# Residual of the first two w_o groups by accumulating transfers, (0,0) of the other two by VectorE, and S1 of the last SwiGLU's first two groups put together by transfers

## The chip, the cores and the metric

The kernel runs on one core of a Trainium2 chip. The metric is the device time of one execution in microseconds. A core has TensorE (the profile writes PE for its matmuls and PEld for its weight loads), VectorE (DVE), ScalarE (ACT), GpSimd (POOL) and SyncE (SP). Each of them works through its own instructions strictly in the order in which they were issued to it. Transfers are issued from SP's queue (plain copies) and from POOL's queue (here: copies that add to what stands in the destination), and are carried by 16 DMA engines that all queues share.

## What is computed

One encoder block over 1024 tokens of width 1024, all in float32:

```python
h = h + 0.5 * swiglu_ffn(rmsnorm(h, norm_ffn1), ffn1_w_in, ffn1_w_out)
u = rmsnorm(h, norm_mix)
...                                   # retention and pooling branches, gates
merged = gate[:, :, 0] * (ret @ w_ret_up) + gate[:, :, 1] * (pool_out @ w_pool_up)
h = h + merged @ w_out
h = h + 0.5 * swiglu_ffn(rmsnorm(h, norm_ffn2), ffn2_w_in, ffn2_w_out)
return rmsnorm(h, norm_final)

def swiglu_ffn(x, w_in, w_out):
    gate, up = split(x @ w_in, 2)
    return (silu(gate) * up) @ w_out
```

The change is about the line with `w_out` (the kernel calls the matrix w_o), its residual addition, and the first products of the last SwiGLU with `ffn2_w_in`.

## The kernel before

**Products.** All large matrix products are done in blocks of 2 by 2 by Strassen's method in Winograd's form: seven block products instead of eight. `strassen` (L479) makes one group: a pair of 128-row weight tiles (`wa`, `wb`, each 128 x 1024, halves L11, L12, L21, L22) against an operand whose sums (R11, R12, T1, T2, T3, T4 and so on) are shared by all groups of a stage. The weights of a group need their own sums: S1 = L21 + L22, S2 = S1 - L11, S3 = L11 - L21, S4 = L12 - S2. A group has seven steps, numbered 0 to 6: L11 x R11, S2 x T2, S1 x T1, S3 x T3, L12 x R21, S4 x R22, L22 x T4. Since TensorE here multiplies in a reduced form of float32, each factor is split into a high part (a cast by ScalarE, L164) and a low part (a subtraction by VectorE, L165), and each product is three matmuls: high x high (L184), high x low (L185) and low x high (L186). A step is 4 x 3 matmuls.

**Results of a group.** Four blocks (tile, half): (0,0) after step 4, (1,1) after steps 2 and 3, (1,0) after step 6, (0,1) after step 5. `evac` adds what lies in PSUM and what was set aside, and writes the block to SBUF. (0,0) and (0,1) come out of PSUM whole; (1,0) and (1,1) are a sum of PSUM and of a set-aside piece. After step 0 the bank `a` is copied by ScalarE into a bank `b` (L530) before step 4 may go on adding to `a`.

**The stage around the change.** `merge` (L1908) runs the four groups of the branch projection (tiles ru0 to ru3, operand "ru"), then the four groups of w_o (`out_group`, L1855, tiles wo0 to wo3, operand "mg", made of the ru tiles), then the last SwiGLU begins (`ffn_in`, groups c0, c11, c1, c12, ..., operand "n3", made of the wo tiles; "n3ssq" collects the squares for its norm). `two_by_two` (L707) takes the groups in pairs and goes through the steps in the order BY_OPERAND = 0, 4, 1, 3, 2, 6, 5, each step for both groups of the pair. The weights of a step are prepared LOOK = 4 steps ahead. `handed` (L1886) puts the making of the next operand into the list of side work (`Flow`), which is emptied two items per step; `m` numbers in it are steps again (0: R11, 4: R21, 1: T2, 3: T3, 2: T1, 6: T4, 5: R22). `rest` is the part that is left to the end of the second pair.

**The residual of w_o.** The block is added to h1 (in HBM). Two ways are in use: the old values are loaded by SP into the block's place in the tile beforehand, and VectorE adds to them (L1879, for blocks of two pieces also L1881); or the block is written without them (ScalarE's copy L1875, VectorE's sum L1873), and a transfer from POOL's queue adds h1 to it (`onto`), after which the next step of the block (`ffn2.quarter`: store to h2, square, sum of squares) must wait; it is kept in `waiting` until `handed` releases it. Before, the second way is used for (0,0) of all four groups and for (1,1) of groups 2 and 3.

**What sets the order.** The names above say in which order work is given out; a scheduler then moves instructions within each engine's queue by its own costs and priorities (evacuations are marked urgent), so the order on each engine is that of the built program. Weight tiles have 5 buffers, raw weight tiles 4 (`raw`), tiles of tag `tl` 4.

Of the kernel before, what the change touches and what calls it, by code (L numbers as in the profile page):

```python
# [21 lines left out]
H = S // 2  # L22
DFF = 2816
FT = DFF // P
FH = FT // 2
# [65 lines left out]
def block_kernel(ctx: ExitStack, tc, x, x_tok, x_two, vecs, f1_in, f1_out, w_in, w_v, pool_w, w_ret, w_pool, w_o,  # L91
# [384 lines left out]
    class Group(list):  # L476
        pass

    def strassen(nx, wa, wb, name, evac, end, begin=None, shared=(), dest=None):  # L479

        t = {}

        def blocks():
            ra, rb = raw(f"{name}ra"), raw(f"{name}rb")
            load(ra, wa)
            load(rb, wb)
            t.update(L11=half(ra, 0), L12=half(ra, 1), L21=half(rb, 0), L22=half(rb, 1))

        def combine(n, a, b, op):
            t[n] = c2(f"{name}{n}")
            tt(t[n], t[a], t[b], op)

        def prep_w(n):
            def go():
                if n == "L11":
                    blocks()
                elif n in ("S2", "S3") and "S1" not in t:
                    combine("S1", "L21", "L22", ADD)  # L500
                if n == "S2":
                    combine("S2", "S1", "L11", SUB)
                elif n == "S3":

                    t["S3"] = t["L21"]
                    tt(t["S3"], t["L11"], t["L21"], SUB)
                if n == "S4" or 3 in shared and n == "S1":

                    t["S4"] = t["S2"]
                    tt(t["S4"], t["L12"], t["S2"], SUB)  # L510
                t["w", n] = weights(t[n], f"{name}w{n}")

            return go

        def prod(dst, w, m, start, stop):
            for i in range(4):
                mm3(t[dst], parts(t["w", w], i), moving(nx.operand(m, i)), start and i == 0, stop and i == 3)

        def u(n):
            t[n] = c2(f"{name}{n}")  # L520
            return t[n]

        def b1():
            if begin:
                begin()
            t["a"] = bank(f"{name}a")
            prod("a", "L11", "R11", True, False)
            t["b"] = sum_bank(f"{name}b")
            with soon():
                copy(t["b"], t["a"])  # L530

        def b6():
            prod("b", "S2", "T2", False, False)
            with soon():
                copy(u("v"), t["b"])

        def fourth():

            if "b5" in t and "p7" in t:
                with soon():  # L540
                    evac((1, 1), t["b"], t["p7"])

        def b5():
            prod("b", "S1", "T1", False, False)
            t["b5"] = True
            fourth()

        def b7():
            t["e"] = bank(f"{name}e")
            prod("e", "S3", "T3", True, False)  # L550
            with soon():
                copy(u("p7"), t["e"])
            fourth()

        def b2():
            prod("a", "L12", "R21", False, True)
            with soon():
                evac((0, 0), t["a"], None)

        def b3():  # L560
            prod("b", "S4", "R22", False, True)
            with soon():
                evac((0, 1), t["b"], None)

        def b4():
            prod("e", "L22", "T4", False, True)
            with soon():
                evac((1, 0), t["e"], t["v"])

        def last(f):  # L570
            def go():
                f()
                t["ends"] = t.get("ends", 0) + 1
                if t["ends"] == 2:
                    end()

            return go

        g = Group([(prep_w("L11"), b1), (prep_w("S2"), b6), (prep_w("S1"), b5), (prep_w("S3"), b7),
                   (prep_w("L12"), b2), (prep_w("S4"), last(b3)), (prep_w("L22"), last(b4))])  # L580
        g.t, g.name, g.dest = t, name, dest
        g.finish = {3: last(lambda: evac((0, 1), t["b"], dest((0, 1)))), 2: lambda: evac((0, 0), t["a"], dest((0, 0)))}
        return g
# [171 lines left out]
    def ffn_in(nx, w, ops, name, ahead, start=None):  # L755

        R, T, B, T4 = ops
        hid = {}

        def group(g):  # L760
            gate_up = {}

            def dest(which):
                tile, j = which
                if tile not in gate_up:
                    gate_up[tile] = (tl if start and g == 0 else t4)(f"{name}{'gu'[tile]}{g}")
                return half(gate_up[tile], j)

            later = []

            def evac(which, in0, in1):
                tile, j = which
                dst, rms = dest(which), nx.rb
                if in1 is not None:
                    tt(dst, in0, in1, ADD)
                elif not tile and rms is not None:
                    tt(dst, in0, half(rms, j), MUL)
                    return
                else:
                    copy(dst, in0)  # L780
                if not tile:
                    later.append(j)

            def end():
                gate, up = gate_up[0], gate_up[1]

                def scale():
                    if len(later) == 2:
                        tt(gate, gate, nx.rms(), MUL)
                    else:  # L790
                        for j in later:
                            tt(half(gate, j), half(gate, j), half(nx.rms(), j), MUL)

                def times(j):
                    tt(half(up, j), half(gate, j), half(up, j), MUL)

                flow.add(scale, lambda: act(gate, gate, AF.Silu), lambda: times(0), lambda: times(1))
                hid[g] = up
                k = g % FH
                if g < FH:  # L800
                    return
                lo, hi, e = hid.pop(k), up, {}
                R11, R12, R21, R22 = half(lo, 0), half(lo, 1), half(hi, 0), half(hi, 1)

                def w1():

                    e["n"], e["m"] = gate, c2(f"{name}m{k}")
                    tt(half(e["n"], 0), R12, R11, SUB)

                def w1b():  # L810
                    tt(half(e["n"], 1), R22, R12, SUB)
                    load(B[k], e["n"])

                def w2():
                    tt(R12, R22, half(e["n"], 0), SUB)
                    load(R[k], lo)
                    load(T[k], hi)

                def w3():
                    tt(e["m"], R21, R12, SUB)  # L820
                    load(T4[k], e["m"])
                    done.add(k)

                flow.add(w1, w1b, w2, w3)

            if start and g == 0:
                return plain_group(nx, start, f"{name}{g}_", evac, end)
            return lambda shared: strassen(nx, w[g, 0], w[g, 1], f"{name}{g}_", evac, end, shared=shared, dest=dest)

        done = ops_done.setdefault(name, set())  # L830
        order = [g for k in range(FH) for g in (k, k + FH)]
        if start:

            return chain(group(0), pairs_of_both(nx, (group(g) for g in order[1:]), BY_OPERAND, 3, ahead))
        return pairs_of_both(nx, (group(g) for g in order), BY_OPERAND, 2, ahead)


# [1017 lines left out]
    def out_group(i):  # L1855
# [3 lines left out]
        def begin():  # L1859
            for z in range(2):  # L1860
                pair[z] = t4(f"{name}{z}")
                if i > 1 or z == 0:
                    load(half(pair[z], 1 - z), half(h1[i + 4 * z], 1 - z))
                else:
                    load(pair[z], h1[i + 4 * z])

        def evac(which, in0, in1):
            tile, j = which
            dst = half(pair[tile], j)
            step = lambda: ffn2.quarter(i + 4 * tile, slice(j * H, (j + 1) * H), pair[tile])  # L1870
            if tile == j and (i > 1 or tile == 0):
                if in1 is not None:
                    tt(dst, in0, in1, ADD)  # L1873
                else:
# [11 lines left out]
    def handed(nx, last):  # L1886
# [1 line left out]
        f = after(nx)  # L1888

        def between(pair, n):  # L1890
            if n in (3, 5):
                flow.add(*waiting)
                waiting.clear()
            if pair == 0:
                if n == BY_OPERAND[-1]:
                    flow.add(*(lambda m=m, i=i: m(i) for i in range(2) for m in (nx.r22, nx.sum1, nx.sum3)))
                return
            flow.add(*(lambda i=i: f[n](i) for i in range(2)))

            for m in {3: (0,), 6: (4,)}.get(n, ()):  # L1900
                flow.add(*(lambda i=i: f[m](i) for i in range(2, 4)))
            if n == BY_OPERAND[-1]:
                rest = [lambda m=m, i=i: f[m](i) for m in (1, 3, 2, 6, 5) for i in range(2, 4)]
                last(rest)

        return between
# [203 lines left out]
```

## Time and profile before

| | us |
|---|---|
| median of 3 runs | 2060.94 |
| lowest, highest run | 2059.88, 2061.10 |
| the profiled execution | 2061.32 |
| its span, first to last instruction | 2059.5 |

The stages that matter, by the first matmul of each in the timeline:

| stretch, us from the start | what runs |
|---|---|
| 1373.6 to 1410.3 | w_o, groups 0 and 1 |
| 1410.3 to 1448.1 | w_o, groups 2 and 3 |
| 1448.1 to 1490.6 | last SwiGLU, groups c0 and c11 |

The page lists busy time, instructions and idle time of each engine. A row of the timeline gives start and duration in us, engine, line, operation, destination<-sources without buffer numbers, shape and count, and in brackets how long the engine had been idle and what ended that. A row of the waits gives the waiting engine, tile and line, then what it waited for, then the sum in us, the number of times and the longest.

### The profile page before, as it was taken

What the parts mean: (1) busy time and instruction counts of PE and PEld (TensorE: products, weight loads), DVE (VectorE), ACT (ScalarE), POOL (GpSimd) and SP (SyncE); (2) the same over time, 40 slices, a digit from 0 to 9 for tenths busy, and PEclk for the clock granted to TensorE, in tenths of its full rate; (3) what the DMA queues carried; (4) which work ended last, traced back from release to release, by engine and by line L of the source; (5) the groups of instructions that cost most, each with busy time, mean ns of one, the idle gap of its engine ahead of it and who ended that gap; (6) DMA issues with size and microseconds to landing.
All of it is one profiled execution on the core that took longest, in us unless ns stands there. A gap on an engine that the chain in (4) does not pass through costs nothing.

```text
span 2059.5 us, 29729 instructions
## 1 busy us (share of the span) xinstructions
PE 2041.1 (99%) x10672; PEld 1810.8 (88%) x10672; DVE 1831.4 (89%) x3253; ACT 1092.0 (53%) x2067; POOL 9.1 (0%) x14
## 2 busy tenths in 40 slices
PE   9999999999999999999999999999999999999998
PEld 7888999988888888888888999888889989998887
DVE  8889998998996798989789987899989989899896
ACT  8545444554754554454447753457645545455454
POOL 0000000000000000000000000010000000000000
PEclk9999999999999999999999999999999999999999
DMA  7332424585543343243336667545233232468642
GB/s 245 138 103 77 144 88 144 200 276 194 189 144 115 101 140 106 92 145 127 110 130 219 205 226 272 193 111 163 80 100 131 88 133 88 136 207 276 210 149 97
DMA packets 120259, 313.57 MB, mean 152 GB/s; under 512 B 13360, under 2 KB 17584, under 8 KB 120112
## 3 DMA queue, kind: packets, MB, share of 16 engines
q1 hardware_dynamic: 118096, 308.01, 43.8%
q0 software_dynamic: 1440, 2.62, 0.8%
q8 instruction: 83, 1.36, 0.3%
q10 hardware_dynamic: 576, 1.05, 0.1%
q14 instruction: 64, 0.52, 0.1%
HBM read 220.93 MB, written 90.70 MB: 151 GB/s over the span
## 4 chain that ended last, share of the span: by engine, by line
PE 84%; DVE 10%; ACT 2%; DMA 2%; issue 2%; SPq 0%; ACTq 0%; DVEq 0%
PE a_b L184 2%; PE a_b L186 2%; PE a_b L185 2%; PE c_b L184 2%; PE c_b L185 2%; PE c_b L186 2%; PE a_e L186 2%; PE c_e L186 2%; PE c_e L184 2%; PE a_e L184 2%; PE c_e L185 2%; PE a_e L185 2%; PE a_a L186 1%; PE a_a L184 1%; PE a_a L185 1%
## 5 line engine op out<-in xcount | busy, mean ns | idle before, releaser
L184 PE MATMUL c_b<-n3T,c_wS 128*128 128x512 f32 x176 | 66.8, 380 | 1.7 <-ACT n3T L164 1.7
L185 PE MATMUL c_b<-n3T,c_wS 128*128 128x512 f32 x176 | 66.8, 380 | 0.0
L186 PE MATMUL c_b<-n3T,c_wS 128*128 128x512 f32 x176 | 66.7, 379 | 0.0
L184 PE MATMUL a_b<-n1T,a_wS 128*128 128x512 f32 x168 | 63.7, 379 | 0.0
L185 PE MATMUL a_b<-n1T,a_wS 128*128 128x512 f32 x168 | 63.7, 379 | 0.0
L186 PE MATMUL a_b<-n1T,a_wS 128*128 128x512 f32 x168 | 63.7, 379 | 0.0
L184 PE MATMUL a_a<-n1R,a_wL 128*128 128x512 f32 x120 | 45.5, 379 | 0.0
L186 PE MATMUL a_a<-n1R,a_wL 128*128 128x512 f32 x120 | 45.5, 379 | 0.0
L185 PE MATMUL a_a<-n1R,a_wL 128*128 128x512 f32 x120 | 45.5, 379 | 0.0
L184 PE MATMUL c_a<-n3R,c_wL 128*128 128x512 f32 x112 | 42.7, 381 | 0.7 <-ACT c_b L530 0.5
L185 PE MATMUL c_a<-n3R,c_wL 128*128 128x512 f32 x112 | 42.4, 379 | 0.0
L186 PE MATMUL c_a<-n3R,c_wL 128*128 128x512 f32 x112 | 42.4, 379 | 0.0
L184 PEld LDWEIGHTS c_b<-n3T,c_wS 128*128 128x128 f32 x176 | 33.3, 189 | 6.6 <-ACT n3T L164 2.1
L185 PEld LDWEIGHTS c_b<-n3T,c_wS 128*128 128x128 f32 x176 | 33.3, 189 | 4.8 <-DVE n3T L165 0.3
L186 PEld LDWEIGHTS c_b<-n3T,c_wS 128*128 128x128 f32 x176 | 33.3, 189 | 4.7
L186 PEld LDWEIGHTS a_b<-n1T,a_wS 128*128 128x128 f32 x168 | 31.8, 189 | 4.5
L184 PEld LDWEIGHTS a_b<-n1T,a_wS 128*128 128x128 f32 x168 | 31.8, 189 | 4.4
L185 PEld LDWEIGHTS a_b<-n1T,a_wS 128*128 128x128 f32 x168 | 31.8, 189 | 4.4
L165 DVE TENSOR_TENSOR a_wS<-a_S,a_wS 128x512 fp32r<-128x512 f32 x45 | 30.6, 682 | 3.6 <-ACT a_wS L164 3.6
L165 DVE TENSOR_TENSOR c_wS<-c_S,c_wS 128x512 fp32r<-128x512 f32 x46 | 31.3, 683 | 2.6 <-ACT c_wS L164 2.6
L184 PE MATMUL c_e<-n3T,c_wS 128*128 128x512 f32 x88 | 33.5, 380 | 0.0
L184 PE MATMUL c_e<-n3T,c_wL 128*128 128x512 f32 x88 | 33.4, 380 | 0.0
(3167 smaller groups left out, 8003.7 us busy)
## 6 DMA issues: line engine op xcount, KB each, us to landing
c_ra<-in_f_in SPq DMA_DIRECT2D x22, 512.0 KB, 3.6
c_rb<-in_f_in SPq DMA_DIRECT2D x22, 512.0 KB, 3.6
a_ra<-in_f_in SPq DMA_DIRECT2D x21, 512.0 KB, 3.7
a_rb<-in_f_in SPq DMA_DIRECT2D x21, 512.0 KB, 3.7
t<-au SPq DMA_DIRECT2D x11, 512.0 KB, 2.8
b<-ag SPq DMA_DIRECT2D x11, 512.0 KB, 3.8
r<-au SPq DMA_DIRECT2D x11, 512.0 KB, 3.5
bra<-in_f_out SPq DMA_DIRECT2D x11, 512.0 KB, 4.8
```

The costliest lines, as they stand in the source:

```text
L165: tt(lo, src, hi.bitcast(F32), SUB)
L184: mm(dst, w[0], m[0], start=start, stop=False, skip_group_check=True)
L185: mm(dst, w[0], m[1], start=False, stop=False, skip_group_check=True)
L186: mm(dst, w[1], m[0], start=False, stop=stop, skip_group_check=True)
```

## The change

In `out_group`, all four blocks of groups 0 and 1 are now written without the residual, and transfers from POOL's queue add it: ten such transfers in w_o instead of six. For groups 2 and 3, (0,0) is now added by VectorE to loaded values, as (0,1) and (1,0) were already; only (1,1) is still by transfer. `handed` releases the waiting blocks at other points, makes the first sums of the n3 operand (r22, sum1, sum3) of groups 0 and 1 later (after step 4 of the second pair and no longer at the end of the first), and puts R22 of groups 0 and 1 into `rest` behind T2 and T3; the last also holds for the mg operand. In `strassen`, the new argument `summed` lets c0 and c11 take S1 from two transfers: one loads L21 of the weights into a half of a `tl` tile (c0_S1), one adds L22, so that VectorE's sum falls away.

```diff
--- before.py
+++ after.py
@@ -476,7 +476,7 @@
     class Group(list):
         pass
 
-    def strassen(nx, wa, wb, name, evac, end, begin=None, shared=(), dest=None):
+    def strassen(nx, wa, wb, name, evac, end, begin=None, shared=(), dest=None, summed=None):
 
 
 
@@ -487,6 +487,13 @@
             load(ra, wa)
             load(rb, wb)
             t.update(L11=half(ra, 0), L12=half(ra, 1), L21=half(rb, 0), L22=half(rb, 1))
+            if summed is not None:
+                if not summed:
+                    s = tl(f"{name}S1")
+                    summed.extend((half(s, 1), half(s, 0)))
+                t["S1"] = summed.pop()
+                load(t["S1"], wb[:, :H])
+                onto(t["S1"], wb[:, H:])
 
         def combine(n, a, b, op):
             t[n] = c2(f"{name}{n}")
@@ -755,7 +762,7 @@
     def ffn_in(nx, w, ops, name, ahead, start=None):
 
         R, T, B, T4 = ops
-        hid = {}
+        hid, halves = {}, []
 
         def group(g):
             gate_up = {}
@@ -825,7 +832,8 @@
 
             if start and g == 0:
                 return plain_group(nx, start, f"{name}{g}_", evac, end)
-            return lambda shared: strassen(nx, w[g, 0], w[g, 1], f"{name}{g}_", evac, end, shared=shared, dest=dest)
+            return lambda shared: strassen(nx, w[g, 0], w[g, 1], f"{name}{g}_", evac, end, shared=shared, dest=dest,
+                                           summed=halves if not start and g % FH == 0 else None)
 
         done = ops_done.setdefault(name, set())
         order = [g for k in range(FH) for g in (k, k + FH)]
@@ -1859,16 +1867,16 @@
         def begin():
             for z in range(2):
                 pair[z] = t4(f"{name}{z}")
-                if i > 1 or z == 0:
+                if i > 1:
                     load(half(pair[z], 1 - z), half(h1[i + 4 * z], 1 - z))
-                else:
-                    load(pair[z], h1[i + 4 * z])
+                    if not z:
+                        load(half(pair[z], z), half(h1[i], z))
 
         def evac(which, in0, in1):
             tile, j = which
             dst = half(pair[tile], j)
             step = lambda: ffn2.quarter(i + 4 * tile, slice(j * H, (j + 1) * H), pair[tile])
-            if tile == j and (i > 1 or tile == 0):
+            if i < 2 or tile and j:
                 if in1 is not None:
                     tt(dst, in0, in1, ADD)
                 else:
@@ -1888,19 +1896,21 @@
         f = after(nx)
 
         def between(pair, n):
-            if n in (3, 5):
+            if (pair, n) in ((0, 3), (1, 4), (1, 5)):
                 flow.add(*waiting)
                 waiting.clear()
-            if pair == 0:
-                if n == BY_OPERAND[-1]:
-                    flow.add(*(lambda m=m, i=i: m(i) for i in range(2) for m in (nx.r22, nx.sum1, nx.sum3)))
+            if (pair, n) == ((1, 4) if nx is ffn2 else (0, BY_OPERAND[-1])):
+                flow.add(*(lambda m=m, i=i: m(i) for i in range(2) for m in (nx.r22, nx.sum1, nx.sum3)))
+            if not pair:
                 return
-            flow.add(*(lambda i=i: f[n](i) for i in range(2)))
+            if n != BY_OPERAND[-1]:
+                flow.add(*(lambda i=i: f[n](i) for i in range(2)))
 
             for m in {3: (0,), 6: (4,)}.get(n, ()):
                 flow.add(*(lambda i=i: f[m](i) for i in range(2, 4)))
             if n == BY_OPERAND[-1]:
-                rest = [lambda m=m, i=i: f[m](i) for m in (1, 3, 2, 6, 5) for i in range(2, 4)]
+                rest = [lambda m=m, i=i: f[m](i) for m, at in ((1, 2), (3, 2), (5, 0), (2, 2), (6, 2), (5, 2))
+                        for i in (at, at + 1)]
                 last(rest)
 
         return between
```

VectorE's rows just ahead of the low part of wo1's S2 weights (wo1wS2), in w_o, groups 0 and 1. mgT.. and mgR22.. are operand parts, wo0rb/wo1S.. sums of weights. Before:

```order
L493 TENSOR_TENSOR wo1S1_13682<-wo1rb_13566 128x512
L165 TENSOR_TENSOR mgT22_13673<-ru20_13295,mgT22_13673 128x512
L165 TENSOR_TENSOR mgT23_13679<-ru30_13331,mgT23_13679 128x512
L493 TENSOR_TENSOR wo1S2_13684<-wo1S1_13682,wo1ra_13565 128x512
L351 TENSOR_TENSOR ru20_13295<-ru21_13297,ru20_13295 128x512
L351 TENSOR_TENSOR ru30_13331<-ru31_13333,ru30_13331 128x512
L165 TENSOR_TENSOR wo1wS2_13686<-wo1S2_13684,wo1wS2_13686 128x512
```

And now:

```order
L165 TENSOR_TENSOR mgT32_13675<-ru20_13295,mgT32_13675 128x512
L351 TENSOR_TENSOR ru30_13331<-ru31_13333,ru30_13331 128x512
L500 TENSOR_TENSOR wo1S1_13682<-wo1rb_13566 128x512
L513 TENSOR_TENSOR wo0rb_13543<-wo0ra_13542,wo0rb_13543 128x512
L165 TENSOR_TENSOR mgT33_13679<-ru30_13331,mgT33_13679 128x512
L500 TENSOR_TENSOR wo1S2_13684<-wo1S1_13682,wo1ra_13565 128x512
L165 TENSOR_TENSOR mgR220_13706<-ru01_12945,mgR220_13706 128x512
L165 TENSOR_TENSOR mgR221_13709<-ru11_12988,mgR221_13709 128x512
L165 TENSOR_TENSOR mgT12_13730<-mgt12_13638,mgT12_13730 128x512
L165 TENSOR_TENSOR wo1wS2_13686<-wo1S2_13684,wo1wS2_13686 128x512
```

Counted from the last row that both programs have in the same place (ru3h01, the gating of ru3's last block), 16 rows stand ahead of wo1wS2 before and 20 now: mgT32, mgT33, wo0rb and mgT12 have come ahead of it, and mgR220 and mgR221, which stood ahead of it anyway, have moved close to it.

ScalarE's rows ahead of the copy of bank a to bank b for wo2 (wo2b<-wo2a). n3q.. and n3ssq are squares of finished wo blocks, wo3wL12 and wo2wS2 high parts of weights. Before:

```order
L291 ACTIVATE n3q4_0_13913<-wo01_13653 128x512
L164 CAST wo2wL12_13941<-wo2ra_13891 128x512
L291 ACTIVATE n3q5_0_13938<-wo11_13691 128x512
L164 CAST wo3wL12_13961<-wo3ra_13916 128x512
L291 ACTIVATE n3q0_512_13958<-wo00_13651 128x512
L291 ACTIVATE n3q1_512_13978<-wo10_13689 128x512
L164 CAST wo2wS2_13986<-wo2S2_13984 128x512
L530 COPY wo2b_14006<-wo2a_13993 128x512
```

And now:

```order
L291 ACTIVATE n3ssq_13839<-wo01_13658 128x512
L164 CAST wo3wL11_13906<-wo3ra_13902 128x512
L164 CAST wo2wL12_13923<-wo2ra_13881 128x512
L346 ACTIVATE wo01_13658<-wo01_13658,vec_66 128x512
L1883 COPY wo00_13657<-wo0b_13672 128x512
L164 CAST wo3wL12_13940<-wo3ra_13902 128x512
L1883 COPY wo10_13689<-wo1b_13704 128x512
L164 CAST wo2wS2_13961<-wo2S2_13959 128x512
L537 COPY wo2b_13982<-wo2a_13969 128x512
```

The four squares of blocks (1,0) and (0,1) have gone to later places; the evacuations of (0,1) of groups 0 and 1 stand there as ScalarE's copies, and the square of wo01 and its scaling, which use a block that a transfer from POOL completes, stand further ahead.

VectorE's rows around the low parts of R21 for tiles 2 and 3 (n3R212, n3R213), at the end of w_o and the start of c0 and c11. Before:

```order
L1879 TENSOR_TENSOR wo31_14020<-wo3e_14152,wo31_14020 128x512
L165 TENSOR_TENSOR c0_wL12_14271<-c0_ra_14223,c0_wL12_14271 128x512
L1881 TENSOR_TENSOR wo31_14020<-wo31_14020,wo3v_14121 128x512
L169 SCALAR_TENSOR_TENSOR n3R212_14373<-wo21_13991,vec_66,n3R212_14373 128x512
L1879 TENSOR_TENSOR wo20_13989<-wo2b_14006,wo20_13989 128x512
L165 TENSOR_TENSOR c11_wL12_14291<-c11_ra_14247,c11_wL12_14291 128x512
L303 TENSOR_TENSOR n3ssq_13843<-n3ssq_13843,n3q7_0_14308 128x512
L493 TENSOR_TENSOR c0_S1_14311<-c0_rb_14224 128x512
```

And now:

```order
L165 TENSOR_TENSOR c11_wS2_14325<-c11_S2_14323,c11_wS2_14325 128x512
L303 TENSOR_TENSOR n3ssq_13839<-n3ssq_13839,n3q7_0_14361 128x512
L392 SCALAR_TENSOR_TENSOR wo11_13690<-wo11_13690,vec_66,wo10_13689 128x512
L165 TENSOR_TENSOR n3T40_14365<-wo01_13658,n3T40_14365 128x512
L165 TENSOR_TENSOR c0_wS3_14347<-c0_rb_14199,c0_wS3_14347 128x512
L165 TENSOR_TENSOR n3T41_14369<-wo11_13690,n3T41_14369 128x512
L169 SCALAR_TENSOR_TENSOR n3R212_14372<-wo21_13967,vec_66,n3R212_14372 128x512
L169 SCALAR_TENSOR_TENSOR n3R213_14378<-wo31_13994,vec_66,n3R213_14378 128x512
```

n3R212 stood ahead of the evacuation of (0,1) of wo2 (wo20<-wo2b); now it stands 12 rows behind that of wo3, and the low parts of c0's and c11's S2 and of T4 come first. TensorE's order has followed: the matmuls with n3R212 and n3R213 of c0 and c11, which were the 31st to the 48th of these groups, now begin with the 36th and end with the 50th, and those with T22 begin with the 78th instead of the 59th, behind T30 and T31 and the sums of squares (n3sum).

## Prediction

> **What bounds the kernel now.** First the page's line of busy times, beside its span:
>
> ```profile
> span 2059.5 us, 29729 instructions
> PE 2041.1 (99%) x10672; PEld 1810.8 (88%) x10672; DVE 1831.4 (89%) x3253; ACT 1092.0 (53%) x2067; POOL 9.1 (0%) x14
> ```
>
> TensorE is busy for 2041.1 of 2059.5 us and the change takes no matmul away, so only TensorE's waits can go. The view of waits for TensorE, cut to 1375 to 1530 us, holds all that lie near the change:
>
> ```profile
> PE c_b L184 <- ACT n3T L164: 1.7, 1, 1.7
> PE wo2a L184 <- ACT wo2b L530: 1.3, 1, 1.3
> PE c_a L184 <- ACT c_b L530: 0.5, 1, 0.5
> PE c_y L184 <- ACT n3R L164: 0.4, 1, 0.4
> PE wo0e L186 <- DVE wo0wS L165: 0.2, 1, 0.2
> ```
>
> They sum to 4.1 us, but matmuls overlap, and a wait costs more than its idle time. The timeline at the second row:
>
> ```profile
> 1415.31 0.38 PE L186 MATMUL wo3a<-mgR,wo3wL 128*128 128x512 f32 x1
> 1416.94 0.48 PE L184 MATMUL wo2a<-mgR,wo2wL 128*128 128x512 f32 x1 [1.25 <-ACT wo2b L530]
> 1417.26 0.38 PE L185 MATMUL wo2a<-mgR,wo2wL 128*128 128x512 f32 x1
> 1417.47 0.38 PE L186 MATMUL wo2a<-mgR,wo2wL 128*128 128x512 f32 x1
> ```
>
> Undisturbed starts are 0.21 to 0.22 apart (1417.26 to 1417.47). Here they are 1.63 apart and then 0.32: lost 1.41 + 0.10 = 1.51, that is the idle time plus 0.26. So the rows cost: c_b 2.0, wo2a 1.5, c_a 0.8, c_y 0.6, wo0e 0.45; a second wait of c_a, too short for this list, is seen below (0.4). **The ceiling of any gain is 5.7 us**, to 2055.6 from the profiled execution's own 2061.3 (span 2059.5 and 1.8 around it). Why these waits are there the view of stretches tells:
>
> ```profile
> 1375.00:1500.00 125.00, 121.17 (x563) 104.08 (x562) 120.19 (x206) 81.91 (x148) 5.23 (x6) 1.00 0.39 117
> ```
>
> The third busy time is VectorE's, 120.19 of 125 us: its queue is full, and ScalarE, whose casts and copies alternate with it in order, is late whenever it is. TensorE's clock is full (1.00).
>
> **The change part by part.** *VectorE's instructions.* For groups 0 and 1, five additions each become two; for groups 2 and 3, four become five; c0 and c11 lose one each. That is 10 + 8 - 4 - 10 + 2 = 6 fewer. Two neighbouring rows give the price:
>
> ```profile
> 1375.24 0.68 DVE L1843 TENSOR_TENSOR ru3h<-ru3b,rg 128x512 f32<-128x512 f32 x1
> 1375.84 0.68 DVE L165 TENSOR_TENSOR mgR<-ru,mgR 128x512 fp32r<-128x512 f32 x1
> ```
>
> One per 0.60 us, so 3.6 us of room on VectorE. It is worth something only where TensorE waits. ScalarE's two (0,0) copies of groups 2 and 3 become two (0,1) copies of groups 0 and 1: nothing in sum.
>
> *wo1's S2 weights: a new wait.* By the order, wo1wS2 moves from the 17th to the 21st row behind ru3h01. VectorE's queue had no gap in this stretch:
>
> ```profile
> 1376.40 0.57 ACT L530 COPY wo0b<-wo0a 128x512 f32<-128x512 f32 x1 [1.78 <-PE wo0a L186]
> 1378.79 0.38 PE L184 MATMUL wo0a<-mgR,wo0wL 128*128 128x512 f32 x1
> 1385.60 0.69 DVE L165 TENSOR_TENSOR wo1wS<-wo1S,wo1wS 128x512 fp32r<-128x512 f32 x1
> 1386.99 0.38 PE L186 MATMUL wo1b<-mgT,wo1wS 128*128 128x512 f32 x1
> 1389.21 0.69 DVE L165 TENSOR_TENSOR wo0wS<-wo0rb,wo0wS 128x512 fp32r<-128x512 f32 x1
> 1389.95 0.48 PE L186 MATMUL wo0e<-mgT,wo0wS 128*128 128x512 f32 x1 [0.18 <-DVE wo0wS L165]
> ```
>
> The last two rows show that a matmul can start 0.74 after its low part starts. So at 1385.60 there were 0.65 to spare (1386.99 - 1385.60 - 0.74), and four rows take 2.4: TensorE waits 1.75. ScalarE adds a little earlier: it must now cast mgT22 before it copies wo0b. Its source is VectorE's third row behind ru3h01 (1375.24 + 3 x 0.60, done 0.7 to 0.8 later at 1377.8); with 0.52 for the cast and 0.57 for the copy the bank is free near 1378.9, where step 4 was due at 1378.79: 0.2 to 0.3, which the wait at wo1b then takes in. Each restart costs 0.1 more (above). Together **+1.8**. The wait at wo0e then goes, since TensorE is late there: **-0.45**.
>
> *The wait at wo2a.* ScalarE's rows ahead of it:
>
> ```profile
> 1413.62 0.75 ACT L291 ACTIVATE n3q<-wo 128x512 f32<-128x512 f32 x1 [1.36 <-DVE wo L1879]
> 1415.78 0.62 ACT L164 CAST wo2wS<-wo2S 128x512 fp32r<-128x512 f32 x1 [1.41 <-DVE wo2S L493]
> 1416.30 0.58 ACT L530 COPY wo2b<-wo2a 128x512 f32<-128x512 f32 x1
> ```
>
> The copy waited behind a square and a cast that waited for VectorE. Now wo2S2 is VectorE's 2nd row behind wo1wS4, some 12 us earlier, and the squares are gone from there; the copy follows TensorE's step 0 of wo2 directly: **-1.5**. What is late next are transfers: ScalarE now stands at n3ssq<-wo01 until POOL's addition to (1,1) of wo0 has landed, and then at wo01's scaling until its store is out.
>
> ```profile
> wo<-h POOLq DMA_DIRECT2D x6, 256.0 KB, 4.0
> h<-wo SPq DMA_DIRECT2D x16, 256.0 KB, 2.0
> wo3rb<-in_w_o SPq DMA_DIRECT2D x1, 512.0 KB, 6.1
> ```
>
> VectorE writes the block near 1400.0, so it lands near 1404.4 and the store near 1406.5; seven ScalarE rows of 0.5 to 0.65 follow (3.7), so the copy could end at 1410.2. TensorE asks for it at 1415.5 + 1.8 - 0.45 = 1416.9. Cover: 6.7 us. In a crowd the additions can take longer; I bound one by 4.0 from below and by 6.1 + 4.0 from above (the wo2 and wo3 weights, 2 MB, are in flight then, and the last of them took 6.1), and take 5: still nothing.
>
> *c0 and c11.* The waits there:
>
> ```profile
> 1447.91 0.38 PE L186 MATMUL wo3b<-mgR,wo3wS 128*128 128x512 f32 x1
> 1451.45 0.68 DVE L1879 TENSOR_TENSOR wo<-wo3b,wo 128x512 f32<-128x512 f32 x1
> 1452.84 0.62 ACT L164 CAST c_wS<-c_S 128x512 fp32r<-128x512 f32 x1 [2.25 <-DVE c_S L493]
> 1453.37 0.58 ACT L530 COPY c_b<-c_a 128x512 f32<-128x512 f32 x1
> 1454.00 0.48 PE L184 MATMUL c_a<-n3R,c_wL 128*128 128x512 f32 x1 [0.53 <-ACT c_b L530]
> 1456.98 0.48 PE L184 MATMUL c_a<-n3R,c_wL 128*128 128x512 f32 x1
> 1463.06 0.62 ACT L164 CAST n3T<-wo 128x512 fp32r<-128x512 f32 x1 [1.72 <-DVE wo L353]
> 1463.73 0.48 PE L184 MATMUL c_b<-n3T,c_wS 128*128 128x512 f32 x1 [1.74 <-ACT n3T L164]
> ```
>
> VectorE takes up wo3's last block at 1451.45, 3.2 us after the bank was full (1447.91 + 0.38). Everything behind inherits that: c0's S2, and behind its cast the copy c_b (0.8 + 0.4 lost), and T2 of tiles 2 and 3 (2.0 + 0.1). With six instructions fewer and S1 gone from this place, VectorE is paced by TensorE's ends of step there; I follow its rows from the evacuation of wo2's (0,1) and find it 1.2 behind at wo3's. So c0's S2 and both copies are in time: -1.2. T2: 24 rows (of 0.60, and 0.67 where scaled) lie between that evacuation and n3T22's low part, 15.5 us, so it starts 16.7 behind wo3b's end and serves at 17.4; TensorE now asks for it 17.8 behind, as T30, T31 and n3sum come first: -2.1. Against these stand two new waits. n3R212 is 12 rows behind, so ScalarE's cast, in order behind that of T41, ends 8.2 behind wo3b's end, where TensorE asks at 7.4: 0.8, and 0.1 each for the restart and the low part. And n3T12 now stands on ScalarE behind its table load:
>
> ```profile
> 1475.34 1.28 ACT L452 ACT_TABLE_LOAD   x1
> ```
>
> Placed by ScalarE's rows it comes 0.7 late: 0.8 with the restart; 0.3 more for n30b and the low parts behind. Together -3.3 + 2.1 = **-1.2**. For these four I have no row, only sums along two queues; each may be 0 or 1.5, so the part lies between -3.3 and +1.
>
> *S1 and SP's queue.* By the order the loads of S1 stand on SP between the last gate load (rg1_01) and wo0ra, and the two additions on POOL behind ru30's:
>
> ```profile
> 1349.59 0.87 POOL L143 DMA_DIRECT2D ru<-pm  x1 [1.37 <-ACT ru3wS L164]
> 1356.31 0.33 SPq L140 DMA_DIRECT2D wo0ra<-in_w_o  x1
> ```
>
> ru30's block is the last that reads the `tl` tile which S1 takes over, so the loads go out near 1349.6, 6.7 us before wo0ra, and S1 is whole near 1358, some 90 us before use. All the work of w_o covers it: 0. Without that cover it would hold wo0's weights, microsecond for microsecond. c_y's wait (0.6) keeps the same rows around it: 0.
>
> **Sum:** 1.8 - 0.45 - 1.5 - 1.2 = -1.35. On the profiled execution 2061.3 becomes 2060.0; the median shown is 0.4 below that execution, so I give **2059.6**.
>
> **The rivals.** (1) *The new order costs nothing at wo1 and c.* VectorE would find its sources earlier than I count: then the ceiling holds without c_y, 2060.9 - 5.1 = 2055.8. Against it: VectorE's queue is gapless ahead of wo1wS2, so four rows must show. (2) *Waits only change place.* At c the new waits equal the old: 2060.9 + 1.8 - 0.45 - 1.5 = 2060.8. For it: in-order queues there leave under 1 us of play. (3) *Slower: the additions hold the scalar queue or SP.* c0's weights stand on SP behind the stores of wo0's and wo1's (0,1), and VectorE's c0_rb stands ahead of wo2wS1. If an addition lands over 6 us later than I say, so over 11 us after its issue, each further microsecond is one of TensorE's, at wo2a: 16 us gives +5, 2064.6. Against it: 4.0 in the row above, with VectorE as busy as it will be. [...]
>
> **How the numbers follow.** Forecast 0.55 (its own range 2058.2 to 2061.0), rival 2 0.22, rival 1 0.11, rival 3 0.12, half of it over 0.2%. A measurement here can tell about 0.2% (4.1 us) from no change: below 2056.8 faster, above 2065.1 slower. Faster 0.09 (most of rival 1), slower 0.06, same 0.85. The range takes the forecast, rival 2, and the near parts of 1 and 3: 2056.7 to 2063.0.
>
> **What would show it.** Right: the view of waits lists wo1b behind wo1wS with 1.4 to 1.6, no wo2a, and in c0 and c11 waits at c_a for n3R and at c_b for n3T of under 1 each; additions land in 4 to 6. Wrong: no wait at wo1b (the row count does not carry), a wait at wo2a whose releaser is ScalarE behind an addition, or VectorE idle ahead of c0_rb for a transfer.

## The result and the profile after

| | us |
|---|---|
| before, median of 12 runs (lowest to highest) | 2060.95 (2059.81 to 2063.76) |
| changed, median of 12 runs (lowest to highest) | 2065.20 (2062.73 to 2068.37) |
| ratio, with its 95% interval | 1.0020 (1.0012 to 1.0028) |
| the changed kernel's profiled execution, its span | 2065.26, 2063.5 |

The changed kernel is slower by 0.2%, some 4.2 us. The busy times and the span, from its page:

```profile
span 2063.5 us, 29734 instructions
PE 2044.5 (99%) x10672; PEld 1812.5 (88%) x10672; DVE 1827.7 (89%) x3247; ACT 1089.7 (53%) x2067; POOL 14.3 (1%) x20
```

VectorE has lost its six instructions (3253 to 3247) and 3.7 us of work. TensorE does the same 10672 products, yet it is busy for 3.4 us more: some of its matmuls have become longer. The view of waits, TensorE's from 1375 to 1530 us:

```profile
PE c_a L185 <- DVE n3R L169: 3.1, 1, 3.1
PE wo1b L184 <- ACT wo1wS L164: 0.6, 1, 0.6
PE c_y L184 <- ACT n3R L164: 0.4, 1, 0.4
PE wo1b L186 <- DVE wo1wS L165: 0.4, 1, 0.4
PE wo2a L184 <- ACT wo2b L537: 0.4, 1, 0.4
PE c_b L184 <- ACT n3T L168: 0.2, 1, 0.2
```

The waits at wo1b are those that were forecast. The first row was not: the first step of c0 stops at its eighth matmul, which waits for the low part of n3R112 (R11 of tile 2). TensorE's timeline there:

```profile
1449.27 0.38 PE L184 MATMUL c_a<-n3R,c_wL 128*128 128x512 f32 x1
1452.74 0.80 PE L185 MATMUL c_a<-n3R,c_wL 128*128 128x512 f32 x1 [3.09 <-DVE n3R L169]
1453.33 0.63 PE L186 MATMUL c_a<-n3R,c_wL 128*128 128x512 f32 x1
1453.75 0.63 PE L184 MATMUL c_a<-n3R,c_wL 128*128 128x512 f32 x1
...
1458.45 0.42 PE L186 MATMUL c_a<-n3R,c_wL 128*128 128x512 f32 x1
1458.70 0.38 PE L184 MATMUL c_a<-n3R,c_wL 128*128 128x512 f32 x1
```

Two losses stand here. Between 1449.27 and 1452.74 are 3.47 instead of 0.22: 3.25 lost. Then the starts are 0.43 apart, twice the usual: from 1452.74 to 1458.70 lie 14 intervals between matmuls, 5.96 where 14 x 0.216 = 3.02 are due (ten intervals, from 1445.82 to 1447.98, took 2.16): 2.94 lost. The view of stretches names the reason, and also where VectorE was before that. Its columns are the stretch, its length, busy time (instructions) of TensorE, of its weight loads, of VectorE, ScalarE and GpSimd, then the granted clock, the DMA share and GB/s. After:

```profile
1400.00:1436.00 36.00, 35.60 (x164) 30.56 (x163) 22.36 (x35) 18.46 (x33) 4.86 (x6) 1.00 0.74 202
1453.00:1458.00 5.00, 5.00 (x12) 3.95 (x13) 5.00 (x9) 2.67 (x5) 0.00 (x0) 0.50 0.14 52
```

Before:

```profile
1400.00:1436.00 36.00, 34.75 (x161) 30.13 (x160) 33.60 (x55) 24.47 (x42) 1.75 (x2) 1.00 0.47 158
```

TensorE's clock was halved (0.50) after its wait. And VectorE, which before had 2.4 us of idle time from 1400 to 1436, now has 13.6, and did 35 instructions there instead of 55. The two largest rows of its waits from 1400 to 1436:

```profile
DVE wo3wL L165 <- ACT wo3wL L164: 7.0, 2, 4.2
DVE c_rb L513 <- DMA c_rb<-in_f_in: 3.6, 1, 3.6
```

And ScalarE, from 1400 to 1416:

```profile
ACT n3ssq L291 <- DMA wo<-h: 6.5, 1, 6.5
ACT wo L346 <- DMA h<-wo: 3.7, 1, 3.7
```

So the chain is: ScalarE stands for 6.5 us at the square n3ssq<-wo01 until the addition to that block has landed, and for 3.7 at its scaling (L346) until the store of the block is out. Behind them in its queue are the high parts of wo3's weights, for whose low parts VectorE waits. Later VectorE waits for c0's second weight tile. From 1436 to 1460 it has no idle time, and n3R112 stands behind all that. (The expectations below put VectorE's idle time at 12.8 and the wait at n3R112 at 4.0; the views say 13.6, and 3.1 with 3.25 lost.)

### The profile page after: what moved, and what is told of

Its sections match the earlier page's. It is cut to its first block, busy times and chain, and to the rows that moved or that the text cites. A ratio compares the mean times of both kernels' runs of the same rounds, so it can differ in the third digit from the quotient of the medians.

```text
span 2063.5 us, 29734 instructions
## 1 busy us (share of the span) xinstructions
PE 2044.5 (99%) x10672; PEld 1812.5 (88%) x10672; DVE 1827.7 (89%) x3247; ACT 1089.7 (53%) x2067; POOL 14.3 (1%) x20
## 4 chain that ended last, share of the span: by engine, by line
PE 83%; DVE 8%; issue 4%; DMA 2%; ACT 2%; POOL 0%; SPq 0%; ACTq 0%; POOLq 0%; DVEq 0%
PE c_b L184 2%; PE c_b L185 2%; PE c_b L186 2%; PE a_b L184 2%; PE a_b L186 2%; PE a_b L185 2%; PE c_e L184 2%; PE c_e L186 2%; PE c_e L185 2%; PE a_e L186 2%; PE a_e L184 2%; PE a_e L185 2%; PE c_a L185 1%; PE c_a L186 1%; PE c_a L184 1%
## 5 line engine op out<-in xcount | busy, mean ns | idle before, releaser
L804 ACT ACTIVATE cg<-cg 128x1024 f32<-128x1024 f32 x22 | 23.2, 1057 | 20.2 <-DVE cg L796 18.8
L164 ACT CAST a_wS<-a_S 128x512 fp32r<-128x512 f32 x45 | 27.3, 621 | 12.0 <-PE a_a L186 7.6
L804 ACT ACTIVATE ag<-ag 128x1024 f32<-128x1024 f32 x22 | 23.3, 1057 | 19.5 <-DVE ag L796 15.0
```

Of the source, the lines that this page charges most:

```text
L164: copy(hi, src)
```

## The experiments

**Theory A**: additions that land late hold ScalarE, VectorE idles behind it and at c0_rb, and is late at c0; the half clock follows from the wait. **Theory B**: the rows that the new order of `handed` puts ahead of n3R112 are too many by themselves. **Theory C**: S1's transfers do it. Each ratio is to the kernel before, run in the same batch (31 or 33 runs of it against seven of "stores by ScalarE" and 11 or 12 of the others); between batches the ratios are compared, not the medians.

| run | median, us | ratio (95%) | VectorE idle, 1400 to 1436 |
|---|---|---|---|
| residual alone | 2061.76 | 1.0002 (0.9993 to 1.0011) | 10.9 |
| S1 alone | 2061.06 | 0.9994 (0.9985 to 1.0003) | 2.9 |
| n3R112 first | 2065.73 | 1.0024 (1.0015 to 1.0033) | 14.1 |
| early loads | 2062.02 | 1.0005 (0.9996 to 1.0014) | 10.4 |
| no additions | 2060.06 | 0.9991 (0.9982 to 0.9999) | 7.7 |
| stores by ScalarE | 2066.94 | 1.0025 (1.0014 to 1.0035) | 13.7 |
| residual alone, early loads | 2058.50 | 0.9989 (0.9980 to 0.9997) | 6.8 |
| early loads, stores by ScalarE | 2063.49 | 1.0010 (1.0002 to 1.0019) | 11.6 |
| S3 from S2 | 2060.77 | 0.9999 (0.9990 to 1.0008) | 10.3 |
| early loads, S3 from S2 | 2058.95 | 0.9990 (0.9981 to 0.9998) | 7.3 |
| the same, mg's R22 as before | 2057.53 | 0.9985 (0.9977 to 0.9994) | 7.5 |
| residual alone, early loads, mg's R22 as before | 2058.98 | 0.9992 (0.9983 to 1.0001) | 7.1 |

### One part of the change at a time

The residual alone: the changed kernel with

```diff
-            return lambda shared: strassen(..., dest=dest,
-                                           summed=halves if not start and g % FH == 0 else None)
+            return lambda shared: strassen(..., dest=dest)
```

> The changed kernel, but S1 of c0 and c11 made by VectorE again. Theory A (late queue: additions and stores that land late hold ScalarE and SP, VectorE stands idle behind them for 12.8 us between 1400 and 1436 and reaches n3R112, the first product of c0, too late; the clock then falls): without S1 by transfers c0_rb is no longer taken up early, so its idle time of 3.6 goes and two additions of 0.6 come in, 2.4 less late: TensorE waits about 1.6 at n3R112 instead of 4.0, too short for the clock to fall, near 2060.9. Theory B (the rows that now stand ahead of n3R112 are too many by themselves, whatever the transfers do): the same rows stand there, 2065. Theory C (S1's transfers are the cause): as before the change, 2061, with no wait at n3R112 and no idle time of ScalarE over 3.

S1 alone: the kernel before with `summed` in `strassen` and `ffn_in` as in the change, and `out_group` and `handed` untouched.

> The kernel before, with S1 of c0 and c11 by transfers alone. Theories A and B: no transfer is late and VectorE has two additions fewer, 2060 to 2061, no wait at TensorE over 2.0. Theory C: 2063 or more.

Neither part is shown to be slower than before; together they are. Theory C falls with the second run, B with the first, where the rows that `handed` puts ahead of n3R112 stand there too and no wait at it is left (A had 1.6 left). TensorE's largest waits in the run with the residual alone:

```profile
PE wo2a L184 <- ACT wo2b L537: 1.2, 1, 1.2
PE c_a L184 <- ACT c_b L537: 0.6, 1, 0.6
```

VectorE's largest, from 1400 to 1436 in the same run:

```profile
DVE wo3wL L165 <- ACT wo3wL L164: 6.9, 2, 3.5
```

The 7 us behind ScalarE are there as in the whole change, but the wait for c_rb is gone. What joins the two parts is a place in memory: S3 = L11 - L21 is written over L21 (c0_rb). While VectorE made S1 out of L21, S3 had to stay behind S1. With S1 from HBM nothing holds it, and it moved 36 rows ahead of n3R112, to a place where its weights were still on the way.

### n3R112 urgent

```diff
             for m in {3: (0,), 6: (4,)}.get(n, ()):
-                flow.add(*(lambda i=i: f[m](i) for i in range(2, 4)))
+                def early(i, m=m):
+                    with soon():
+                        f[m](i)
+                flow.add(*(lambda i=i: early(i) for i in range(2, 4)))
```

> The changed kernel, with n3R112 and n3R113 urgent: on VectorE they stand 9 rows (5.4 us) further ahead, all else in place. Theory B: the wait at n3R112 was the whole loss, it goes with the fall of the clock, 6.2 us: 2059. Theory A: VectorE as a whole is late, so the wait moves to n3R212 (36 products after c0's first; its row starts near 1460.1, TensorE asks near 1455.8): 4 to 5 there, with a fall of the clock again, 2064 to 2066.

Nothing was gained. TensorE's waits:

```profile
PE c_a L184 <- ACT c_b L537: 4.1, 2, 2.1
PE wo2a L184 <- ACT wo2b L537: 1.1, 1, 1.1
PE c_a L184 <- ACT n3R L168: 0.7, 1, 0.7
```

The wait moved, though not to where I put it: it is the copies c0_b and c11_b that are late now (4.1 in two waits), since ScalarE must first cast S2 and waits 3.8 for it. n3R212 has 0.7. The clock stayed full. But the edit moved more than it was meant to. VectorE's rows for c0's S2 (c_S) and for n3R112 and n3R113, in the changed kernel:

```profile
1447.74 0.68 DVE L500 TENSOR_TENSOR c_S<-c_S,c_ra 128x512 f32<-128x512 f32 x1
1451.94 1.41 DVE L169 SCALAR_TENSOR_TENSOR n3R<-wo,vec,n3R 128x512 fp32r<-128x512 f32 x2
```

And with n3R112 urgent:

```profile
1447.35 1.40 DVE L169 SCALAR_TENSOR_TENSOR n3R<-wo,vec,n3R 128x512 fp32r<-128x512 f32 x2
1452.88 0.68 DVE L500 TENSOR_TENSOR c_S<-c_S,c_ra 128x512 f32<-128x512 f32 x1
```

S2 went seven places back as n3R112 went nine forward, so "all else in place" did not hold: the waits at the copies come from this new order. This run therefore says neither that the whole queue was late nor anything against B; B falls with the residual alone.

### The crowd at the first addition

The six loads of old values for groups 2 and 3 (1.5 MB) go out with group 1's beginning:

```diff
         def begin():
             for z in range(2):
-                pair[z] = t4(f"{name}{z}")
-                if i > 1:
-                    load(half(pair[z], 1 - z), half(h1[i + 4 * z], 1 - z))
-                    if not z:
-                        load(half(pair[z], z), half(h1[i], z))
+                pair[z] = olds.pop((i, z)) if i > 1 else t4(f"{name}{z}")
+            if i == 1:
+                for k in range(2, 4):
+                    for z in range(2):
+                        t = olds[k, z] = t4(f"wo{k}{z}")
+                        load(half(t, 1 - z), half(h1[k + 4 * z], 1 - z))
+                        if not z:
+                            load(half(t, z), half(h1[k], z))
```

> The changed kernel, with the six loads of old values for groups 2 and 3 issued ahead of the w_o weights of these groups, in place of behind them, so that 1.5 MB no longer share the DMA engines with the first additions. Theory A, with crowding as the reason for the late landing: the first addition lands in 5 to 6 instead of 8.1, ScalarE's idle time ahead of n3ssq<-wo01 falls from 6.5 to about 4, VectorE's idle time from 12.8 to about 7, TensorE's wait at n3R112 to 0 to 1.5 without a fall of the clock: 2060 to 2061.5. [...] Theory B: 2065.

In the changed kernel SP's queue issues four weight loads and those six around the first addition (the last two 0.2 and 0.8 behind it), 3.5 MB within 5.3 us:

```profile
1395.65 0.33 SPq L140 DMA_DIRECT2D wo2ra<-in_w_o  x1
...
1397.84 3.06 SPq L140 DMA_DIRECT2D wo<-h  x6
```

POOL's queue issues the addition for which ScalarE's square waits:

```profile
1399.64 0.88 POOL L143 DMA_DIRECT2D wo<-h  x1 [12.20 <-DVE wo L1881]
```

It had landed 8.1 after its issue, just before the square began at 1407.80. With early loads it lands in 5.2 (1400.31 to ScalarE's start at 1405.51), ScalarE's wait is 5.2 instead of 6.5, the wait at wo2a is gone, and most of the loss comes back (1.0020 to 1.0005). Against the 4.0 of the kernel before, crowding is the larger part of the late landing: 2.9 of the 4.1 us. What of the gain is the landing's is not separated: the scheduler also moved some rows of VectorE and ScalarE, wo01's scaling ahead of wo2's cast among them. VectorE's idle time fell by 3.2, less than I expected: its wait behind wo3's casts went from 7.0 to 0.9, but its wait at c0_rb grew, and the low part of wo2's weights now waits behind the scaling.

```profile
DVE c_rb L513 <- DMA c_rb<-in_f_in: 4.3, 1, 4.3
DVE wo2wL L165 <- ACT wo2wL L164: 1.8, 1, 1.8
DVE wo3wL L165 <- ACT wo3wL L164: 0.9, 2, 0.6
```

TensorE, which comes to c0 without the delay at wo2a, still waits 2.2 at n3R112.

### No additions at all

```diff
-                onto(dst, half(h1[i + 4 * tile], j))
+                if i > 1:
+                    onto(dst, half(h1[i + 4 * tile], j))
                 waiting.append(step)
```

> The changed kernel without the eight transfers that add h1 to the blocks of w_o's groups 0 and 1: h1 is missing in these blocks; everything else, the stores to h2 too, is there. Theory A: nothing is left that lands late; ScalarE's idle time ahead of n3ssq<-wo01 is under 3 (in place of 6.5), VectorE's idle time from 1400 to 1436 under 4 (in place of 12.8), c0_rb finds its weights, TensorE waits less than 1 at n3R112 and its clock does not fall; what is left is the wait at wo1b of 1.9: 2060 or less. If it stays at 2064 or more, theory A falls.

The whole loss is gone, and a little more. VectorE idles for 7.7, not under 4: ScalarE still waits 3.5 for the store ahead of the scaling. But c0_rb, at the same place in VectorE's queue, finds its weights, n3R112 is in time, and TensorE's longest waits are these:

```profile
PE wo1b L184 <- ACT wo1wS L164: 0.6, 1, 0.6
PE c_a L184 <- ACT n3R L168: 0.5, 1, 0.5
PE wo1b L186 <- DVE wo1wS L165: 0.4, 1, 0.4
```

### Stores from ScalarE's queue, a miss

```diff
-                load(self.keep[mt][:, tokens], src)
+                (nc.scalar.dma_start if self.name == 'n3' else load)(self.keep[mt][:, tokens], src)
```

> The changed kernel, with the stores of w_o's blocks to h2 issued from ScalarE's queue in place of SP's, so that SP is free for c0's and c11's weights. Theory A: these weights land before 1412, VectorE's idle time of 3.6 at c0_rb goes, that behind ScalarE (4.2 + 2.8) stays; 2 to 4 us less late than the changed kernel at n3R112, as in the run without S1 by transfers: 2061 to 2062.5. Rival: ScalarE pays for the twenty issues and waits for stores in its own queue, what SP gains it loses: 2064 to 2066.

The rival was right, and its range (2064 to 2066) still 0.9 too low; the stores are sixteen, not twenty. A store waits for its addition, and on ScalarE's queue everything behind it waits too, here the copy that wo2a needs:

```profile
1422.25 0.57 ACT L537 COPY wo2b<-wo2a 128x512 f32<-128x512 f32 x1 [3.12 <-DMA wo<-h]
```

TensorE's timeline at wo2a:

```profile
1416.42 0.38 PE L186 MATMUL wo3a<-mgR,wo3wL 128*128 128x512 f32 x1
1422.88 0.79 PE L184 MATMUL wo2a<-mgR,wo2wL 128*128 128x512 f32 x1 [6.08 <-ACT wo2b L537]
1423.46 0.63 PE L185 MATMUL wo2a<-mgR,wo2wL 128*128 128x512 f32 x1
```

c0's first weight tile came no earlier either: its load was issued at 1420.64 (1419.53 in the changed kernel), though no store stood ahead of it on SP. It goes into a buffer that VectorE must first be done with: S4 of wo2, its last reader, ended at 1420.57 here, 0.07 ahead of the load, and at 1417.42 in the changed kernel, where the load went 2.1 later, behind a store (1419.11). So SP's stores do hold c0's weights, by some 2 us; that the weights could land before 1412 without them was wrong, since VectorE's own lateness holds them too. With early loads beside it the same edit was tried again:

> The whole change, with the six loads of old values early and the stores to h2 on ScalarE's queue. Theory A: VectorE's idle time at c0_rb (4.3 in the run with early loads) goes, TensorE's wait at n3R112 (2.4) and the fall of the clock with it, 3.5 to 4 less than that run: 2058 to 2059.5, below the kernel before. Rival: ScalarE's issues cost as much, 2061 to 2063.

Nothing of the 3.5 to 4 was gained: the ratio is 1.0010 against 1.0005 with early loads alone, and the two intervals overlap. VectorE's wait at c0_rb did fall, to 1.0, and no wait at n3R112 is left, but TensorE waits 2.1 at wo2a and 1.5 at the copies c0_b and c11_b instead, and the rival's range was again a little low.

### c0_rb put back, and the cures together

S3 equals L22 - S2 too. Made so, it has to follow S2:

```diff
-                    tt(t["S3"], t["L11"], t["L21"], SUB)
+                    if summed is not None:
+                        tt(t["S3"], t["L22"], t["S2"], SUB)
+                    else:
+                        tt(t["S3"], t["L11"], t["L21"], SUB)
```

> The whole change, but S3 of c0 and c11 made as L22 - S2 in place of L11 - L21 (the same value up to rounding), so that it has to follow S2: on VectorE c0_rb moves from a place 36 rows ahead of n3R112 to 7 rows behind it, nothing else moves. Theory A: VectorE's idle time of 3.6 at c0_rb goes, n3R112 comes 3 to 4 earlier, TensorE's wait of 4.0 there shrinks to under 1 and the clock does not fall; waits of 1 to 1.5 at c0_b's copies stay: 2060 to 2062. Rival (the place of c0_rb is a symptom: the transfers of S1 themselves, or the other waits, do it): 2064 to 2066.

Moving this one row took the whole loss away (1.0020 to 0.9999), with the additions as late as ever (the first lands in 7.8): VectorE still waits 7.8 behind ScalarE, but not at c_rb, and n3R112 is no longer waited for. From 1380 to n3R112 no other row of VectorE has changed its place in the trace. TensorE's longest waits (those that A left at c0_b's copies did not come):

```profile
PE wo2a L184 <- ACT wo2b L540: 1.3, 1, 1.3
PE c_a L184 <- ACT n3R L168: 0.8, 1, 0.8
```

So the loss needs the hold at c0_rb: without it VectorE's queue bears the late additions. Whether it would bear the hold at c0_rb without them is not shown, since early loads only ease them, and in the run without additions the wait at c0_rb went too. Early loads with the residual alone, and early loads with the whole change and S3 from S2:

> The residual's part of the change alone (S1 by VectorE) with the six loads of old values early. Theory A: both holds are eased, the crowd at the first addition and the early c0_rb: VectorE's idle time from 1400 to 1436 under 5, no wait at n3R112, no fall of the clock; TensorE loses about 0.7 at wo1b, 0.3 at wo2a and 1.7 in c0 and c11: 2059 to 2060.5. Rival: two additions more on VectorE at c0 cost what the early loads gain, 2061 to 2062.

> The whole change with both cures: loads of old values early, and S3 from S2. Theory A: as the run with the residual's part and early loads (2058.5), with two additions less on VectorE: 2057 to 2059, no wait at n3R112, full clock. Rival: 2061 or more.

Both are faster than before, and in the first VectorE still idles for 6.8, not under 5. Last, R22 of the mg operand back where it was, for the wait at wo1b:

```diff
-            if n != BY_OPERAND[-1]:
+            if nx is mg or n != BY_OPERAND[-1]:
                 flow.add(*(lambda i=i: f[n](i) for i in range(2)))
...
-                rest = [lambda m=m, i=i: f[m](i) for m, at in ((1, 2), (3, 2), (5, 0), (2, 2), (6, 2), (5, 2))
+                rest = [lambda m=m, i=i: f[m](i) for m, at in [x for x in ((1, 2), (3, 2), (5, 0), (2, 2), (6, 2), (5, 2)) if nx is not mg or x[1]]
```

> As the run before this one in the list, and R22 of the mg operand where it was before the change (step 1 of the prediction's sum: the four rows ahead of wo1's S2 weights). On VectorE the low part of these weights is again the 17th row behind ru3h01. The prediction's step: the wait at wo1b (0.7 with early loads, 1.9 in the changed kernel) goes and at most 0.45 at wo0e comes back: 0.2 to 0.7 less than without it, 2056.5 to 2058.5. Rival: the rows are not what wo1b waits for, and the wait stays.

> The same two cures with S1 of c0 and c11 by VectorE (early loads, R22 of mg as before): it tells what S1 by transfers is worth once c0_rb is out of the way. VectorE has two additions more, 1.2 us, of which TensorE sees 0 to 1.2: 2057 to 2059; if S1 by transfers is worth nothing, within 0.3 of the run with both.

In the run with both cures and this edit TensorE's waits from 1375 to 1530 are:

```profile
PE c_a L184 <- ACT n3R L168: 0.8, 1, 0.8
PE c_y L184 <- ACT n3R L164: 0.4, 1, 0.4
PE wo0e L186 <- DVE wo0wS L165: 0.2, 1, 0.2
```

wo1b is gone and wo0e is back, as the prediction's first step has it. This version, 2057.53, beats the kernel before by 0.15% and, by the two ratios, the changed one by 0.35%. What S1 by transfers adds to it (2058.98 without) lies within the intervals of the two ratios and stays open.

## Why the prediction was wrong, point by point

- **Six instructions less on VectorE**: right, 3.7 us of busy time. But room on a queue is of use only if the queue can move; VectorE gained 3.7 and lost 11.2 to idle time (13.6 less 2.4).
- **wo1's S2 weights, +1.8**: right in size. The matmuls before and behind the waits at wo1b (1385.76 to 1388.12 below) take 2.36 where four intervals of 0.216 are due: 1.5, and near 0.4 went at the copy wo0b. It came as two waits, as ScalarE's cast was late as well, so the view showed 0.6 and 0.4 where I wrote 1.4 to 1.6. Its cause is shown by the last edit. wo0e's wait went, as forecast.

```profile
1385.76 0.38 PE L186 MATMUL wo0b<-mgT,wo0wS 128*128 128x512 f32 x1
1386.72 0.48 PE L184 MATMUL wo1b<-mgT,wo1wS 128*128 128x512 f32 x1 [0.58 <-ACT wo1wS L164]
1387.04 0.38 PE L185 MATMUL wo1b<-mgT,wo1wS 128*128 128x512 f32 x1
1387.80 0.48 PE L186 MATMUL wo1b<-mgT,wo1wS 128*128 128x512 f32 x1 [0.39 <-DVE wo1wS L165]
1388.12 0.38 PE L184 MATMUL wo1b<-mgT,wo1wS 128*128 128x512 f32 x1
```

- **wo2a, -1.5, with a cover of 6.7**: the cover was eaten. The copy wo2b ended at 1416.46, not at 1410.2, as the two waits of ScalarE took 10.2 together. Of -1.5 came about -0.6: a wait of 0.4 at wo2a stays, and wo3's copy behind it costs 0.3 more.
- **Where it failed**: "I bound one by 4.0 from below and by 6.1 + 4.0 from above, ... and take 5: still nothing". The size 8.1 lay within that bound. The mistake was the second half: I held the late landing only against the copy wo2b. The casts of wo3's weights stand on ScalarE behind the same square, and VectorE waits for them. The step on c0 and c11 then went on as if VectorE were "paced by TensorE's ends of step there". It had 11 us more of idle time behind it. So -1.2 became +3.8: 3.25 + 2.94 lost at n3R112, and the remaining 2.4 saved as the old waits at c_a and c_b shrank.
- **The sum, stretch by stretch**, each from its first matmul to that of the next: groups 0 and 1 of w_o took 38.13 instead of 36.73 (+1.4, forecast +1.35), groups 2 and 3 took 37.20 instead of 37.78 (-0.6, forecast -1.5), and from c0's first matmul to the first on c_y it was 72.83 instead of 69.05 (+3.8, forecast -1.2). Together that is +4.6. The spans differ by 4.0 only, since the changed kernel's profiled execution came to w_o 0.96 earlier (1372.65 against 1373.61). Those of the other runs come to it between 1372.2 and 1377.2, so this lead is spread and no gain of the change.
- **A row not followed**: I counted rows to n3R212 and n3T22, which c0 asks for later, and not to n3R112, which it asks for first. Followed with a VectorE that is never idle, it would have named only the place and not the price: it came 3.25 late with 11.2 us more of idle time ahead of it. That is an argument; the run with n3R112 urgent does not show it.
- **S1 by transfers, 0**: right alone, wrong in company. I priced its own arrival (in time by far) and not what VectorE's missing S1 lets go: S3, which moved ahead to a place where its weights had not come. This term failed as much as the one on the additions: with S3 put back the loss is gone. I named c0_rb as a sign, not as a cost.
- **The rivals**: the third had the mechanism (additions hold ScalarE; SP's order at c0_rb) and nearly the time, 2064.6, but from 11 us of landing on and at wo2a. It set in at 8.1, through VectorE, at c0, so that its time is near the measured one by luck. The fall of the clock, 2.9 us in the profiled execution, no rival had.

## What to carry to other kernels

When a transfer takes over an engine's work, price the wait for its landing at each engine that stands behind the waiting instruction, to the second and third hand, not at the one consumer that was late before. Idle time given to a full in-order queue may be paid at a later place where that queue is on the path, here 20 to 40 us later. How much of it the queue makes up has to be followed row by row: 10.9 us cost nothing with the residual alone, while 10.4 us with early loads left a wait of 2.2. And where an instruction is taken away, look at what it had held back by its buffer: what becomes free to run early may go to a place where its input is not there.

## What the runs showed of the hardware

TensorE's clock fell after a wait. After 3.09 us of idle time the starts were 0.43 apart for 5.7 us, which nearly doubled the price of the wait (3.25, then 2.94 more). With early loads a wait of 2.24 was enough, and the fall came later. The timeline of that run:

```profile
1449.93 0.48 PE L185 MATMUL c_a<-n3R,c_wL 128*128 128x512 f32 x1 [2.24 <-DVE n3R L169]
1450.25 0.38 PE L186 MATMUL c_a<-n3R,c_wL 128*128 128x512 f32 x1
...
1451.35 0.63 PE L185 MATMUL c_a<-n3R,c_wL 128*128 128x512 f32 x1
1451.78 0.63 PE L186 MATMUL c_a<-n3R,c_wL 128*128 128x512 f32 x1
...
1454.76 0.38 PE L184 MATMUL c_a<-n3R,c_wL 128*128 128x512 f32 x1
```

For 1.4 us the matmuls ran at full speed, then for 3.4 at half. Two waits of about 2.0 in the run with n3R112 first, 3.65 apart, did nothing to the clock (1.00 from 1448 to 1490). By the granted clock of short stretches the half rate lasted 3.4 with early loads and twice that, 6.8, in the changed kernel (from 1451.68, still in the wait, to 1458.51). The next change in that trace is at 2059.26, so the changes lie 6.83 and 600.75 apart: 2 and 176 times 3.413.

The length of a wait alone did not decide it. Between 1300 and 1540 the clock fell in four of the 14 executions. Here they are, and beside them three with waits near 2 us in which it did not fall:

| run | waits, us | clock after it |
|---|---|---|
| stores by ScalarE | 6.08 | half |
| changed | 3.09 | half |
| early loads | 2.24 | half |
| residual alone, early loads, mg's R22 as before | 2.07 | half |
| early loads, stores by ScalarE | 2.10 | full |
| n3R112 first | 2.01, 2.08 | full |
| S1 alone | 1.78 | full |

A wait of 2.07 halved the clock (mean granted clock of that execution: 0.998), and waits of 2.08 and 2.10 did not (0.999 in both). In the 3.41 us up to the fall TensorE was idle for 60% in the changed kernel (1449.65 to 1451.68) and for 59% with early loads (1447.91 to 1449.93). What decides between half and full is not shown: with 14 executions these are findings of this case and no rule.

The changed kernel's runs spread over 5.6 us, those of before over 4.0. The mean granted clock of the changed kernel's runs is 0.997 in three (2066.9 us in the mean), 0.998 in five (2065.4) and 0.999 in four (2064.1), so the fall of the clock makes part of this spread, and some 3 us of the loss are there without it.

An addition of 256 KB from GpSimd's queue took 0.86 to issue in the changed kernel both with VectorE busy (at 1402.87) and with VectorE idle (at 1405.27). It landed in 4.0 in the kernel before (the median of six) and in 8.1 where 3.5 MB of loads were issued around it.
